# The order of the four input projections in a hybrid layer, with the state-space tables, chunk inputs and kernels moved among the products

## The chip, the cores and the metric

The kernel runs on one core of a Trainium2 chip. A core has five engines, each with its own list of instructions: TensorE (PE: matrix products and transposes, with weight loads in PEld), VectorE (DVE), ScalarE (ACT), GpSimd (POOL) and SyncE (SP, which issues the DMAs here). The metric is the device time of one execution in microseconds; of several runs the median counts.

## The reference

The program computes one layer of a streaming encoder over 1024 positions of 1024 channels in float32. What matters here is its first third:

```
h = x @ w_in                              # 1024 x 1024 @ 1024 x 2048
u, q, k, v, gate = split(h)               # 512, 256, 256, 512, 512 columns
q, k = rotary(q), rotary(k)
# state-space group: 32 groups of 16 channels, a 64-dim complex diagonal state each
bu     = einsum('blgc,gpc->blgp', u, b_bar)
states = associative_scan(a * s + bu)     # over the positions
y_s5   = rms_norm(glu(gelu(Re(C . states) + D * u)))
# retention over chunks, from q, k, v
y_ret  = group_norm(retention(q, k, v)) * silu(gate)
x = layer_norm(alpha * x + concat(y_s5, y_ret) @ w_out)
x = layer_norm(alpha * x + conv_ffn(x))
```

b_bar and the powers of the discretised state matrix are made from the parameters in the kernel. The two layer norms, the output projection and the gated MLP follow; the change does not touch them.

## The kernel before

**Products.** `w_in` is cut into four blocks of 512 columns: block 0 is u, block 1 q and k, block 2 v, block 3 the gate. Each block is one stage of `project()`. x and the weights are held as a high and a low part (an ACT cast, then a DVE subtraction that gives the rest), and each product is done three times: high by high, high by low, low by high. A stage is 8 steps over the inner dimension (k = 0 to 7, two in each of four kp), for 8 output tiles of 128 x 512 (j = 0 to 7), so 8 x 3 x 8 = 192 matmuls, one for each PSUM bank in turn. `load_w` (L168) loads a weight tile (`wraw`), casts it (L183) and splits it (L184) into one of the slots `wsp`.

**Stages in the order of before.** qk (block 1), which also loads and splits x; u (block 0), with the rotary products (L265 to L272, `rot`, `kz`) of the qk banks on DVE and their transposes (`qkt`, L276) on PE among u's products; a block of the state-space part; v (block 2); g (block 3); and then the y products (L623).

**State-space part.** DVE makes the tables: the powers of the state matrix (L331 to L409), then `W` (six instructions of 128 x 2048, L423 to L425), the end tables `ER`, `EIs` (L438 to L445). ACT and DVE copy u out of PSUM into `U` (L297), SP stores it to `uscr` and loads it back in another order as `UT`. PE transposes `W` (`bt`, L452), the copies of that are `BT` (L453), and PE multiplies `UT` by `BT` in eight groups (L461, "V groups"; L471 copies them to `V2`). A scan of seven steps over two halves follows (L501 to L514): ACT swaps the halves of the partitions (`sw`, two copies a step), DVE does four instructions. `scan_carries` (L532 to L535) is a chain of 15 steps of four small instructions, and `scan_correct` (L549 to L553) four times four instructions of 128 x 960. `short_kernel` (L478) is one small matmul for each of the 32 groups into the bank `kern`; it stands among the v products of kp 1, and `between_done` (L489) takes the bank away. As that bank is one of eight, the eighth v tile (`late`) is done afterwards for the first four k. After g, DVE makes the tables `CT` (L599 to L601), which the y products need.

**What sets the order.** The program is written as one stream; the tile framework works out the order of each engine's instructions, with the weight loads of later stages at a higher priority, and puts the semaphores between them. Each engine then runs its list as it stands. PSUM banks are taken in turn (`bank`), SBUF slots from a list of free ones (`Arena`): a tile that gets a slot waits for the last reader of the tile that had it.

Of the kernel before, what the change touches and what calls it, by code (L numbers as in the profile page):

```python
# [20 lines left out]
P = 128  # L21
# [85 lines left out]
def layer_kernel(ctx, tc, a, out):  # L107
# [40 lines left out]
    def x_parts(k):  # L148
        return [slice(0, 128), slice(128, 512), slice(512, SEQ)] if k == 0 else [slice(0, SEQ)]

# [17 lines left out]
    def load_w(blk, kp):  # L168

        n = f"wsp{blk}_{kp}"  # L170
        if blk == 1:
            load_x(kp)
        t = A.get([P, 2, 2, 512], F32R, n)
        rs = []
        for q in range(2):
            wr_n[0] += 1
            r = mp.tile([P, 512], F32, tag=f"wraw{wr_n[0] % 3}", name=f"wraw{blk}_{kp}{q}")
            SP.dma_start(r, a["w_in"][blk, :, 2 * kp + q])
            rs.append(r)
            if blk == 1:  # L180
                load_xk(2 * kp + q)
        for q, r in enumerate(rs):
            S.copy(t[:, q, 0], r)  # L183
            V.tensor_sub(t[:, q, 1], r, f32(t[:, q, 0]))  # L184
            if blk == 1:
                split_xk(2 * kp + q)
        if blk == 1:
            A.free(f"xraw{kp}")
        return t, n


    def project(blk, ops, banks, between=None, after=None, mid=None):


        ws = []
        for kp in range(4):
            with tc.high_priority(0 if blk == 1 else HP):
                w, n = load_w(blk, kp)
            late = between is not None and kp < 2
            todo = deque(between) if late and kp == 1 else ()  # L200
            ws.append(w)
            for q in range(2):
                k = 2 * kp + q
                if k < 7:
                    for (xi_, wi_) in ((0, 0), (0, 1), (1, 0)):
                        for j in range(7 if late else 8):
# [7 lines left out]
            if late:  # L214
                if kp == 0:
                    continue
                after()
                bank_n[0] -= 1
                banks[7] = bank("late")
                for k in range(4):  # L220
# [4 lines left out]
            if blk == 3:  # L225
                A.free(f"x{2 * kp}", f"x{2 * kp + 1}")
            if mid is not None and kp == 1:
                mid()

# [22 lines left out]

    banks = [bank(f"qk{b}") for b in range(8)]
    project(1, ops_b, banks)
    SP.dma_start(con, a["con"])
    SP.dma_start(ident, a["ident"])
    SP.dma_start(gains, a["gains"])
    qkT = [A.get([P, 4, 4, P], F32, f"qkT{h}") for h in range(2)]
    kz = A.get([P, 8, 256], F32, "kz")
    rot = A.get([P, 2, 2, 512], F32, "rot")  # L260
    for b in range(8):
        m1_, m2_ = rot[:, b % 2, 0], rot[:, b % 2, 1]
        cosb = con[:, C_COS + 32 * b:C_COS + 32 * b + 32].unsqueeze(1).broadcast_to([P, 16, 32])
        sinb = cust(con, C_SIN + 64 * b, [[0, 8], [32, 2], [1, 32]])
        V.tensor_mul(m1_.rearrange("p (a f) -> p a f", f=32), banks[b].rearrange("p (a f) -> p a f", f=32), cosb)  # L265
        V.tensor_mul(cust(m2_, 0, [[64, 8], [32, 2], [1, 32]]),
                     cust(banks[b], 32, [[64, 8], [-32, 2], [1, 32]]), sinb)
        V.tensor_add(m1_, m1_, m2_)
        V.tensor_mul(kz[:, b].rearrange("p (h d) -> p h d", h=4), m1_[:, 256:512].rearrange("p (h d) -> p h d", h=4),
                     con[:, C_ZETA:C_ZETA + 4].unsqueeze(2).broadcast_to([P, 4, 64]))  # L270

        V.tensor_mul(m1_[:, 0:256].rearrange("p (h d) -> p h d", h=4), m1_[:, 0:256].rearrange("p (h d) -> p h d", h=4),  # L272
                     con[:, C_XI:C_XI + 4].unsqueeze(2).broadcast_to([P, 4, 64]))
        tb = bank(f"qkt{b}")
        for e in range(4):
            T.transpose(tb[:, e * P:(e + 1) * P], m1_[:, e * P:(e + 1) * P], ident)  # L276
        S.copy(qkT[b // 4][:, b % 4], tb.rearrange("p (e k) -> p e k", e=4))  # L277
    A.free("rot")


    banks = [bank(f"u{j}") for j in range(8)]
    project(0, ops_t, banks)
    par = A.get([P, 2048], F32, "par")
    SP.dma_start(par, a["s5p"][:, 0:2048])
    pw = A.get([P, 2048], F32, "pw")
    par3 = pw[:, 1600:1696]
    SP.dma_start(par3, a["s5p"][:, 2048:S_END])

# [157 lines left out]

    BT = A.get([P, 32, P], F32, "BT")
    for q in range(8):
        b_ = bank(f"bt{q}")
        for e in range(4):  # L450
            g = 4 * q + e
            T.transpose(b_[:, e * P:(e + 1) * P], W[g // 16][:, g % 16].rearrange("p j c -> p (j c)"), ident)  # L452
        (S.copy if q % 2 else V.tensor_copy)(BT[:, 4 * q:4 * q + 4], b_.rearrange("p (g k) -> p g k", g=4))  # L453

    V2 = []
    for h in range(2):
        vb = []
        for q in range(4):
            b_ = bank(f"v{h}{q}")
            for e in range(4):  # L460
                T.matmul(b_[:, e * P:(e + 1) * P], lhsT=BT[:, 16 * h + 4 * q + e], rhs=UT[h][:, 4 * q + e],  # L461
                         start=True, stop=True)
            vb.append(b_)
        if h == 1:
            A.free("BT")
        t = A.get([P, 2, 16, P], F32, f"V2{h}")
        G.memset(t[:, 0, :, 0:1], 0.0)
        for q in range(4):
            v3 = vb[q].rearrange("p (g k) -> p g k", g=4)
            gs = slice(4 * q, 4 * q + 4)  # L470
            S.copy(t[:, 0, gs, 1:P], v3[:, :, 0:P - 1])  # L471
        V2.append(t)

    c1s = par[:, 0:512]
# [9 lines left out]
    V.tensor_mul(d3, d3, con[:, C_DM:C_DM + 16].unsqueeze(1).broadcast_to([P, NG, 16]))  # L484
    A.free("UT0", "UT1")
    tscr = dr.tile([240, 512], F32, name="tscr")
# [31 lines left out]
    def scan_carries():  # L518

        car = par[:, 0:1024].rearrange("p (z g s) -> p z g s", z=2, g=32)  # L520
        for h in range(2):
# [40 lines left out]
    vt = [A.get([P, 4, 512], F32, f"vt{h}") for h in range(2)]  # L562
    for b in range(8):
        S.copy(vt[b // 4][:, b % 4], banks[b])
    car = scan_carries()
# [38 lines left out]
    for h in range(2):  # L604
# [4 lines left out]
        TT.append(t)  # L609
    A.free("par", "pw", "scan")  # L610
    gt = [A.get([P, 4, 512], F32, f"gt{h}") for h in range(2)]
# [736 lines left out]
```

## Time and profile before

| | |
|---|---|
| runs | 1030.85, 1033.16, 1032.67 us; median 1032.67 |
| profiled execution | 1030.58 us |
| its span, first to last instruction | 1028.8 us |
| PE busy | 1003.2 us, 98% of the span |
| DVE busy | 815.4 us, 79% |
| ACT busy | 453.6 us, 44% |
| granted TensorE clock, mean | 0.996 |

The shares are means over stages with different limits. The rows below are therefore of single stretches: the part from the start to the y products is the first 214 us of the span. "x8" in a row is a count of instructions run together; a matmul whose two operands are plain fp32 stands twice in it, so the 32 matmuls of the V groups are "x64".

### The profile page before, as it was taken

How to read it: one execution, taken by the hardware profiler on the slowest of the kernel's cores; microseconds unless marked ns; L12 is line 12 of the kernel's file. 1: busy time of each engine (PE TensorE's matmuls, PEld its weight loads, DVE VectorE, ACT ScalarE, POOL GpSimd, SP SyncE). 2: the span in 40 equal slices, each digit the busy share in tenths (PEclk: the TensorE clock that was granted, in tenths of full speed). 3: DMA queues.
4: the chain of work that ended last, by engine and by line, in shares of the span. 5: the costliest groups of instructions: out<-in, count | busy, mean ns of one | idle time of the engine just before them, and what ended most of it. 6: DMA issues, size and time to landing. Idle time of an engine off the chain costs nothing.

```text
span 1028.8 us, 12777 instructions
## 1 busy us (share of the span) xinstructions
PE 1003.2 (98%) x4748; PEld 829.6 (81%) x4748; DVE 815.4 (79%) x1385; ACT 453.6 (44%) x763; POOL 50.1 (5%) x60
## 2 busy tenths in 40 slices
PE   9999899999999999999999999999999999999996
PEld 7887778887787887788888888888888888888885
DVE  5498899947775599999778778778777896759987
ACT  5121663047552147554444444444444445444800
POOL 0000000002211140000000000000000000000003
PEclk9999999999999999999999999999999999999998
DMA  8402511151212222144132232232223985643113
GB/s 285 153 1 64 193 40 54 61 206 67 98 44 102 82 103 93 52 154 144 72 128 108 74 130 103 91 114 103 106 99 143 322 323 207 233 143 123 42 41 122
DMA packets 41934, 124.05 MB, mean 121 GB/s; under 512 B 4384, under 2 KB 10912, under 8 KB 37520
## 3 DMA queue, kind: packets, MB, share of 16 engines
q1 hardware_dynamic: 41584, 122.72, 33.7%
q8 instruction: 37, 0.61, 0.2%
q10 hardware_dynamic: 288, 0.52, 0.1%
q14 instruction: 25, 0.20, 0.1%
HBM read 92.06 MB, written 31.16 MB: 120 GB/s over the span
## 4 chain that ended last, share of the span: by engine, by line
PE 82%; DVE 8%; ACT 4%; issue 2%; POOL 2%; DMA 1%; POOLq 0%; SPq 0%; DVEq 0%; ACTq 0%
PE dn L133 6%; PE dn L135 6%; PE dn L134 6%; PE u L208 4%; PE qk L208 4%; PE g L208 4%; PE v L208 1%; PE wb L133 1%; PE wb L135 1%; PE wb L134 1%; PE y L623 1%; DVE XT L1201 1%; DVE ring L976 1%; PE wo L135 1%; PE wo L133 1%
## 5 line engine op out<-in xcount | busy, mean ns | idle before, releaser
L975 ACT CAST ring<-wu 128x512 fp32r<-128x512 f32 x131 | 80.6, 620 | 145.2 <-DMA wu<-in_w_up_dram 14.5
L976 DVE TENSOR_TENSOR ring<-wu,ring 128x512 fp32r<-128x512 f32 x131 | 91.4, 702 | 21.8 <-ACT ring L975 21.8
L134 PE MATMUL dn<-ring 128*128 128x512 f32 x264 | 102.9, 390 | 0.0
L133 PE MATMUL dn<-ring 128*128 128x512 f32 x264 | 102.8, 389 | 0.0
L135 PE MATMUL dn<-ring 128*128 128x512 f32 x264 | 102.8, 389 | 0.0
L975 ACT CAST ring<-araw 128x512 fp32r<-128x512 f32 x66 | 41.1, 623 | 74.4 <-PE dn L134 61.7
L976 DVE TENSOR_TENSOR ring<-araw,ring 128x512 fp32r<-128x512 f32 x66 | 45.6, 693 | 27.6 <-ACT ring L975 27.6
L134 PEld LDWEIGHTS dn<-ring 128*128 128x128 f32 x264 | 49.6, 188 | 10.5 <-DVE ring L976 0.2
L135 PEld LDWEIGHTS dn<-ring 128*128 128x128 f32 x264 | 49.6, 188 | 10.3
L133 PEld LDWEIGHTS dn<-ring 128*128 128x128 f32 x264 | 49.6, 188 | 10.2
L976 DVE TENSOR_TENSOR ring<-wd,ring 128x512 fp32r<-128x512 f32 x66 | 45.2, 690 | 1.0 <-ACT ring L975 1.0
L975 ACT CAST ring<-wd 128x512 fp32r<-128x512 f32 x66 | 40.5, 617 | 8.2 <-DVE wd L1141 4.4
L208 PE MATMUL v<-wsp,x 128*128 128x512 f32 x147 | 42.7, 410 | 1.1 <-ACT V L471 1.1
L208 PE MATMUL qk<-wsp,x 128*128 128x512 f32 x168 | 40.8, 404 | 0.9 <-ACT x L162 0.9
L208 PE MATMUL u<-x,wsp 128*128 128x512 f32 x168 | 40.1, 394 | 0.0
L208 PEld LDWEIGHTS qk<-wsp,x 128*128 128x128 f32 x168 | 32.5, 195 | 9.1 <-ACT x L162 2.5
L208 PE MATMUL g<-wsp,x 128*128 128x512 f32 x168 | 38.2, 389 | 0.0
L208 PEld LDWEIGHTS g<-wsp,x 128*128 128x128 f32 x168 | 31.5, 188 | 6.5
L208 PEld LDWEIGHTS u<-x,wsp 128*128 128x128 f32 x168 | 30.8, 188 | 6.6 <-ACT qkT L277 0.6
L183 ACT CAST wsp<-wraw 128x512 fp32r<-128x512 f32 x32 | 19.4, 620 | 34.7 <-DMA wraw<-in_w_in_dram 23.5
L208 PEld LDWEIGHTS v<-wsp,x 128*128 128x128 f32 x147 | 27.4, 189 | 6.1 <-ACT V L471 1.9
L1068 DVE SCALAR_TENSOR_TENSOR cg<-Ab,cv,cg 128x1024 f32<-128x1024 f32 x22 | 28.3, 1285 | 4.8 <-ACT cg L1067 4.8
(1141 smaller groups left out, 2697.1 us busy)
## 6 DMA issues: line engine op xcount, KB each, us to landing
wu<-in_w_up_dram SPq DMA_DIRECT2D x22, 1024.0 KB, 4.8
araw<-hd SPq DMA_DIRECT2D x33, 512.0 KB, 3.7
wraw<-in_w_in_dram SPq DMA_DIRECT2D x32, 256.0 KB, 3.8
hd<-cg SPq DMA_DIRECT2D x22, 256.0 KB, 2.0
hd<-cg SPq DMA_DIRECT2D x11, 512.0 KB, 2.6
hd<-sS SPq DMA_DIRECT2D x11, 512.0 KB, 2.8
wd<-in_w_down_dram SPq DMA_DIRECT2D x11, 512.0 KB, 5.6
wd<-in_w_down_dram SPq DMA_DIRECT2D x22, 256.0 KB, 5.2
```

Source lines behind the costliest of these rows:

```text
L133: T.matmul(o, lhsT=lh, rhs=rh, start=first, stop=False)
L134: T.matmul(o, lhsT=lh, rhs=rl, start=False, stop=False)
L135: T.matmul(o, lhsT=ll, rhs=rh, start=False, stop=last)
L183: S.copy(t[:, q, 0], r)
L208: T.matmul(banks[j], lhsT=l, rhs=r, start=(k == 0 and xi_ == 0 and wi_ == 0), stop=False)
L623: T.matmul(o, lhsT=UT[h][:, gl], rhs=TT[h][:, :, 16 * gl:16 * gl + 16], start=True, stop=False)
L975: S.copy(t[:, 0], src)
L976: V.tensor_sub(t[:, 1], src, f32(t[:, 0]))
L1068: V.scalar_tensor_tensor(c, Ab[:, 1:1025], cv[:, f, 1:2], c, ALU.mult, ALU.add)
L1201: V.tensor_sub(lo[:, ks], src[:, ks], f32(hi[:, ks]))
```

## The change

The stages now stand in the order u, v, qk, g. x is loaded and split in the u stage, its first tile in two pieces instead of three. The constants are loaded in the middle of the u stage. The eight transposed groups of `W` and the eight V groups, which were a block of their own, now stand among the products of v, one after every fifth product: the transposes in kp 0, the V groups in kp 1. They share one PSUM bank (`small`), so v has seven banks of its own until its `late` tile; ACT alone copies them out. The kern matmuls move to kp 1 of the qk stage, and the rotary products and their transposes follow qk. `car`, the array of the carries, gets a slot of its own and no longer lies in `par`.

```diff
-        return [slice(0, 128), slice(128, 512), slice(512, SEQ)] if k == 0 else [slice(0, SEQ)]
+        return [slice(0, 512), slice(512, SEQ)] if k == 0 else [slice(0, SEQ)]
...
-    def project(blk, ops, banks, between=None, after=None, mid=None):
+    def project(blk, ops, banks, between=(), after=None, mid=None):
...
-            todo = deque(between) if late and kp == 1 else ()
+            todo = deque(between[kp]) if late and kp < 2 else deque()
...
-                after()
-                bank_n[0] -= 1
-                banks[7] = bank("late")
+                if after is not None:
+                    after()
+                banks[7] = small("late")
...
+    def small(name):
+
+        if bank_n[0] == small_n[0]:
+            bank_n[0] -= 1
+        b_ = bank(name)
+        small_n[0] = bank_n[0]
+        return b_
+
+    def spread_out(groups, n):
+
+        return [g for gr in groups for g in [gr] + [lambda: None] * (n - 1)]
...
-    banks = [bank(f"qk{b}") for b in range(8)]
-    project(1, ops_b, banks)
...
     banks = [bank(f"u{j}") for j in range(8)]
-    project(0, ops_t, banks)
...
+    project(0, ops_t, banks, mid=load_constants)
...
-    for q in range(8):
-        b_ = bank(f"bt{q}")
+    def make_BT(q):
+        b_ = small(f"bt{q}")
         for e in range(4):
...
-        (S.copy if q % 2 else V.tensor_copy)(BT[:, 4 * q:4 * q + 4], b_.rearrange("p (g k) -> p g k", g=4))
+        S.copy(BT[q // 4][:, 4 * (q % 4):4 * (q % 4) + 4], b_.rearrange("p (g k) -> p g k", g=4))
...
+    def make_V(i):
+        h, q = i // 4, i % 4
+        b_ = small(f"v{h}{q}")
+        for e in range(4):
+            T.matmul(b_[:, e * P:(e + 1) * P], lhsT=BT[h][:, 4 * q + e], rhs=UT[h][:, 4 * q + e], start=True, stop=True)
+        S.copy(V2[h][:, 0, 4 * q:4 * q + 4, 1:P], b_.rearrange("p (g k) -> p g k", g=4)[:, :, 0:P - 1])
...
+    banks = [bank(f"v_{b}") for b in range(7)] + [None]
+    project(2, ops_b, banks, [spread_out([partial(make_BT, q) for q in range(8)], 5),
+                              spread_out([partial(make_V, i) for i in range(8)], 5)])
...
-        car = par[:, 0:1024].rearrange("p (z g s) -> p z g s", z=2, g=32)
+        car = A.get([P, 1024], F32, "car").rearrange("p (z g s) -> p z g s", z=2, g=32)
...
-    banks = [bank(f"v_{b}") for b in range(7)] + [None]
-    kb = bank("kern")
-    project(2, ops_b, banks, [partial(short_kernel, g) for g in range(NG)], between_done)
...
+    banks = [bank(f"qk{b}") for b in range(7)] + [None]
+    kb = small("kern")
+    project(1, ops_b, banks, [[], [partial(short_kernel, g) for g in range(NG)]], between_done)
```

On PE, between u and v: before, the transposes (`bt`) of `W` and the V groups (`v_879` and so on, from `UT` and `BT`) stand in one block behind u's last products.

```order
L233 MATMUL u_459<-x_306,wsp_3_631 128x512 x3
L452 MATMUL bt_831<-ident,W_793 128x128 x4
L452 MATMUL bt_837<-ident,W_793 128x128 x4
L452 MATMUL bt_843<-ident,W_793 128x128 x4
L452 MATMUL bt_849<-ident,W_793 128x128 x4
L452 MATMUL bt_855<-ident,W_798 128x128 x4
```

After, on PE in the same place, each group of transposes stands between products of v (`v_505` to `v_511` are its seven banks).

```order
L208 MATMUL v_510<-wsp_0_512,x_100 128x512
L446 MATMUL bt_522<-ident,W_462 128x128 x4
L208 MATMUL v_511<-wsp_0_512,x_100 128x512
L208 MATMUL v_505<-wsp_0_512,x_100 128x512
L208 MATMUL v_506<-wsp_0_512,x_100 128x512
L208 MATMUL v_507<-wsp_0_512,x_100 128x512
L446 MATMUL bt_533<-ident,W_462 128x128 x4
```

The block is gone from PE's list; its 16 groups now have products on either side.

On ACT, at the end of the scan, before: the copies of the last scan steps (`V<-V`), then the casts of the next stage's weights (`wsp`), then the copies of v out of its banks (`vt`).

```order
L501 COPY V_925<-V_925 64x256
L502 COPY V_925<-V_925 64x256
L183 CAST wsp_0_1395<-wraw_00_1396 128x512
L183 CAST wsp_0_1395<-wraw_01_1398 128x512
L183 CAST wsp_1_1452<-wraw_10_1453 128x512
L183 CAST wsp_1_1452<-wraw_11_1455 128x512
L564 COPY vt_1297<-v_1023 128x512
```

After, on ACT at the end of the scan, where the next stage is qk and `wsp_0_947` holds its first weights.

```order
L498 COPY V_503<-V_503 64x256
L499 COPY V_503<-V_503 64x256
L470 COPY vt_837<-v_505 128x512
L470 COPY vt_837<-v_506 128x512
L470 COPY vt_837<-v_507 128x512
L470 COPY vt_837<-v_508 128x512
L470 COPY vt_838<-v_509 128x512
L470 COPY vt_838<-v_510 128x512
L470 COPY vt_838<-v_511 128x512
L183 CAST wsp_0_947<-wraw_00_948 128x512
```

The copies of v have moved ahead of the first cast for the next stage, behind the scan's last copies.

On DVE, behind the carries, before: the corrections (`scan<-par,pw`, `V<-V,scan`) follow without anything between.

```order
L535 TENSOR_TENSOR par<-par,scan 128x64
L550 TENSOR_TENSOR scan<-par,pw 128x960
L549 TENSOR_TENSOR scan<-par,pw 128x960
L551 TENSOR_TENSOR scan<-scan 128x960
L553 TENSOR_TENSOR V_899<-V_899,scan 128x8x120
L550 TENSOR_TENSOR scan<-par,pw 128x960
```

After, on DVE in the same place, where `rot` and `kz` are the rotary products from the banks `qk_939` and `qk_940`.

```order
L532 TENSOR_TENSOR car<-car,scan 128x64
L547 TENSOR_TENSOR scan<-car,pw 128x960
L546 TENSOR_TENSOR scan<-car,pw 128x960
L548 TENSOR_TENSOR scan<-scan 128x960
L566 TENSOR_TENSOR rot<-qk_939,con 128x512
L567 TENSOR_TENSOR rot<-qk_939,con 128x512
L566 TENSOR_TENSOR rot<-qk_940,con 128x512
L569 TENSOR_TENSOR rot<-rot 128x512
```

The rotary products now stand behind the carries and among the corrections.

## Rows read from the trace of the kernel before

**Rows 1.** Waits of PE: line, what it waited for, total us, times, longest

```profile
PE bt L452 <- DVE W L425: 4.7, 1, 4.7
PE late L233 <- DVE par L489: 1.9, 1, 1.9
...
PE v L208 <- ACT V L471: 1.1, 1, 1.1
```

**Rows 2.** Busy us of each engine in three stretches, with granted clock

```profile
core 0: us, PE busy (x) PEld busy (x) DVE busy (x) ACT busy (x) POOL busy (x), PEclk, DMA share, GB/s
0.00:52.00 52.00, 49.93 (x204) 39.99 (x204) 25.71 (x37) 19.53 (x27) 0.87 (x7) 1.00 0.63 217
100.00:110.00 10.00, 5.27 (x36) 5.05 (x35) 9.04 (x16) 4.46 (x8) 0.00 (x0) 0.83 0.99 332
150.00:214.00 64.00, 64.00 (x284) 52.99 (x283) 59.42 (x98) 14.53 (x25) 0.00 (x0) 1.00 0.25 87
```

**Rows 3.** PE in time order, 99 to 128: start, us, instruction, idle before

```profile
99.26 1.91 PE L452 MATMUL bt<-ident,W 128*128 128x128 f32 x16
105.90 3.27 PE L452 MATMUL bt<-ident,W 128*128 128x128 f32 x16 [4.73 <-DVE W L425]
109.01 7.31 PE L461 MATMUL v<-UT,BT 128*128 128x128 f32 x64
...
127.36 0.29 PE L478 MATMUL kern<-par,W 128*128 128x16 f32 x2
```

**Rows 4.** PE in time order, 141 to 215

```profile
141.55 3.24 PE L208 MATMUL v<-wsp,x 128*128 128x512 f32 x13
...
170.66 38.24 PE L208 MATMUL g<-wsp,x 128*128 128x512 f32 x168
...
214.18 0.38 PE L623 MATMUL y<-TT,UTb 128*128 128x128 f32 x2
```

**Rows 5.** DVE in time order, 46 to 85: rotary products, tables, W

```profile
46.89 0.69 DVE L265 TENSOR_TENSOR rot<-qk,con 128x512 f32<-128x512 f32 x1 [8.20 <-PE qk L233]
...
69.03 0.18 DVE L331 TENSOR_SCALAR scr<-pw 128x32 f32<-128x32 f32 x1 [1.30 <-PE qkt L276]
...
82.52 2.28 DVE L423 TENSOR_TENSOR W<-pw,par 128x2048 f32<-128x2048 f32 x1
```

**Rows 6.** ACT in time order, 106 to 133: casts, V copies, scan copies

```profile
106.07 0.62 ACT L183 CAST wsp<-wraw 128x512 fp32r<-128x512 f32 x1 [2.96 <-DMA uscr<-U]
...
115.34 0.66 ACT L501 COPY V<-V 64x256 f32<-64x256 f32 x1
...
118.62 2.03 ACT L471 COPY V<-v 128x508 f32<-128x508 f32 x4
...
128.81 0.68 ACT L501 COPY V<-V 64x256 f32<-64x256 f32 x1 [1.06 <-DVE V L514]
...
132.64 0.68 ACT L501 COPY V<-V 64x256 f32<-64x256 f32 x1 [1.05 <-DVE V L514]
```

**Rows 7.** DVE in time order, 145 to 212: carries, corrections, CT

```profile
145.99 0.68 DVE L489 TENSOR_TENSOR par<-par,kern 128x512 f32<-128x512 f32 x1
...
152.38 0.26 DVE L532 TENSOR_TENSOR scan<-par,pw 128x64 f32<-128x64 f32 x1
...
168.47 1.96 DVE L550 TENSOR_TENSOR scan<-par,pw 128x960 f32<-128x960 f32 x1
...
172.33 1.16 DVE L551 TENSOR_TENSOR scan<-scan 128x960 f32<-128x960 f32 x1
...
197.97 4.49 DVE L600 TENSOR_TENSOR CTt<-pw,par 128x2048 f32<-128x2048 f32 x2
...
206.78 4.49 DVE L601 TENSOR_TENSOR CT<-CT,CTt 128x2048 f32<-128x2048 f32 x2
```

**Rows 8.** PE in time order, first products and the end of qk

```profile
5.90 1.65 PE L208 MATMUL qk<-wsp,x 128*128 128x512 f32 x3 [0.53 <-ACT x L162]
7.92 1.65 PE L208 MATMUL qk<-wsp,x 128*128 128x512 f32 x3 [0.37 <-ACT x L162]
...
51.45 1.36 PE L276 MATMUL qkt<-ident,rot 128*128 128x128 f32 x8
```

More of the change, by code (lines that the diff above doesn't have):

```diff
@@ L170, in load_w @@
         n = f"wsp{blk}_{kp}"
-        if blk == 1:
+        if blk == 0:
             load_x(kp)
@@ L179, in load_w @@
             rs.append(r)
-            if blk == 1:
+            if blk == 0:
                 load_xk(2 * kp + q)
@@ L184, in load_w @@
             V.tensor_sub(t[:, q, 1], r, f32(t[:, q, 0]))
-            if blk == 1:
+            if blk == 0:
                 split_xk(2 * kp + q)
-        if blk == 1:
+        if blk == 0:
             A.free(f"xraw{kp}")
         return t, n
-    def project(blk, ops, banks, between=None, after=None, mid=None):
+    def project(blk, ops, banks, between=(), after=None, mid=None):
         ws = []
+        late = len(between) > 0
         for kp in range(4):
-            with tc.high_priority(0 if blk == 1 else HP):
+            with tc.high_priority(0 if blk == 0 else HP):
                 w, n = load_w(blk, kp)
-            late = between is not None and kp < 2
-            todo = deque(between) if late and kp == 1 else ()
+            todo = deque(between[kp]) if late and kp < 2 else deque()
             ws.append(w)
@@ L205, in project @@
                     for (xi_, wi_) in ((0, 0), (0, 1), (1, 0)):
-                        for j in range(7 if late else 8):
+                        for j in range(7 if late and kp < 2 else 8):
                             l, r = ops(w[:, q], k, j, xi_, wi_)
@@ L213, in project @@
                         proj3(banks[j], ops, w[:, q], k, j, False, True)
-            if late:
+            assert not todo
+            if mid is not None and kp == 1:
+                mid()
+            if late and kp < 2:
                 if kp == 0:
                     continue
-                after()
-                bank_n[0] -= 1
-                banks[7] = bank("late")
+                if after is not None:
+                    after()
+                banks[7] = small("late")
                 for k in range(4):
@@ L226, in project @@
                 A.free(f"x{2 * kp}", f"x{2 * kp + 1}")
-            if mid is not None and kp == 1:
-                mid()
+    small_n = [0]
+    def small(name):
[6 more added lines that the diff above has]
+        return [g for gr in groups for g in [gr] + [lambda: None] * (n - 1)]
     def proj3(o, ops, w, k, j, first, last):
@@ L250, in layer_kernel, with load_constants @@
     A.free("zero")
-    banks = [bank(f"qk{b}") for b in range(8)]
-    project(1, ops_b, banks)
[L255 to L278, printed above, removed]
     banks = [bank(f"u{j}") for j in range(8)]
-    project(0, ops_t, banks)
     par = A.get([P, 2048], F32, "par")
-    SP.dma_start(par, a["s5p"][:, 0:2048])
     pw = A.get([P, 2048], F32, "pw")
     par3 = pw[:, 1600:1696]
-    SP.dma_start(par3, a["s5p"][:, 2048:S_END])
+    def load_constants():
+        SP.dma_start(par3, a["s5p"][:, 2048:S_END])
+        SP.dma_start(con, a["con"])
+        SP.dma_start(ident, a["ident"])
+        SP.dma_start(par, a["s5p"][:, 0:2048])
+        SP.dma_start(gains, a["gains"])
+    project(0, ops_t, banks, mid=load_constants)
     uscr = dr.tile([4, P, 1024], F32, name="uscr")
@@ L445, in layer_kernel @@
     V.tensor_scalar(EIs[:, 1], EI, sgm, None, ALU.mult)
-    BT = A.get([P, 32, P], F32, "BT")
-    for q in range(8):
-        b_ = bank(f"bt{q}")
+    BT = [A.get([P, 16, P], F32, f"BT{h}") for h in range(2)]
+    def make_BT(q):
+        b_ = small(f"bt{q}")
         for e in range(4):
@@ L452, in layer_kernel @@
             T.transpose(b_[:, e * P:(e + 1) * P], W[g // 16][:, g % 16].rearrange("p j c -> p (j c)"), ident)
-        (S.copy if q % 2 else V.tensor_copy)(BT[:, 4 * q:4 * q + 4], b_.rearrange("p (g k) -> p g k", g=4))
+        S.copy(BT[q // 4][:, 4 * (q % 4):4 * (q % 4) + 4], b_.rearrange("p (g k) -> p g k", g=4))
     V2 = []
     for h in range(2):
[L457 to L465, printed above, removed]
         t = A.get([P, 2, 16, P], F32, f"V2{h}")
         G.memset(t[:, 0, :, 0:1], 0.0)
[L468 to L471, printed above, removed]
         V2.append(t)
+    def make_V(i):
[7 more added lines that the diff above has]
+                              spread_out([partial(make_V, i) for i in range(8)], 5)])
+    A.free("BT0", "BT1", "UT0", "UT1")
+    vt = [A.get([P, 4, 512], F32, f"vt{h}") for h in range(2)]
+    for b in range(8):
+        S.copy(vt[b // 4][:, b % 4], banks[b])
     c1s = par[:, 0:512]
@@ L609, in layer_kernel @@
         TT.append(t)
-    A.free("par", "pw", "scan")
+    A.free("par", "pw", "scan", "car")
     gt = [A.get([P, 4, 512], F32, f"gt{h}") for h in range(2)]
```

22 lines of the change are left out of this document (19 added, 3 removed).

## The prediction, made before the changed kernel ran

> **What bounds the kernel now.** I read the busy share first (TensorE, PE, is at work for almost the whole span), then what PE waited for, then the windows and time-ordered rows of the first 215 us. From the y products (L623) on, every engine's instructions stand in the order of before, so all that can change is when PE reaches the first of them: 214.18 [rows 4]. PE loses little ahead of it: 4.73 us before the second half of the bt transposes, 1.94 before the late products, 1.08 before a v product [rows 1, 3]. Its clock fell once: after the 4.73 us idle, 16 transposes took 3.27 us where 16 had just taken 1.91 [rows 3], and the granted clock of that window is 0.83 [rows 2], between the levels of 1.2 and 2.4 GHz. That is another 1.36; all four are 9.1 us. Behind PE stands VectorE (DVE): busy 59.42 of the 64 us from 150 to 214 [rows 2], and its last CT instruction ends at 211.27, 2.9 us before the y products [rows 7].
>
> **The prices.** The g stage's 192 products take 170.66 to 214.18, 43.5 us, 0.2267 each [rows 4]. Four transposes cost 1.91/4 = 0.48 [rows 3]. The eight V groups took 7.31, 0.91 each [rows 3]. With 32 kern matmuls among the products, 127.36 to 141.55 is 14.2 us for 31 products, so they add 7.2 [rows 3, 4]. A rope pair of banks is 20.8/4 = 5.2 us on DVE (46.89 to 67.73, where DVE's idle before 69.03 begins) [rows 5]. A pair of scan steps (both halves) is 132.64 - 128.81 = 3.83 [rows 6]; a step of one half alone is not seen before and lies between its two copies on ScalarE (ACT), 2 x 0.68, and the whole pair. I take 3.0, nearer to the pair, because its copies and its DVE instructions wait for each other in turn and only a little of the pair overlaps. Carries are 16.1 us (152.38 to 168.47); CT's six instructions are 13.3, 2.25 each (197.97 to 211.27) [rows 7].
>
> **Part 1, the start: +0.7.** The first x tile's second half came to PE at 7.92, after four products that need only the first [rows 8]. Before, the first four banks lie in that half; of u every second bank lies in the other, so one product is done, not four: 3 x 0.23. The qk stage ended at 51.45, where the qkt transposes start [rows 8]; u ends at 52.3.
>
> **Part 2, between u and v: +3.3.** The old block (bt transposes, then V groups, each waiting for a transfer) goes, and its 4.73, 1.08 and 1.36 with it. Instead the v products start behind u, with a transposed group or a V group after every fifth one. Two things can hold them. The first v weights use the slot that the last W instruction frees, and the odd copies of U on DVE stand behind all six W instructions. DVE was busy 25.71 of the first 52 us [rows 2], 5.1 of it rope; the table work of 69.03 to 82.52 and six W instructions of 2.28 add 27.2 [rows 5]. That is 47.8 of 52 us, with the constants landing only among the x loads, so I put the end of W at 51.9 and of the last U copy at 55.7: bt0 waits 2.05. Free cover gives 0 here, and a chain 5 us later gives 7. Then the casts of the second and third v weights stand on ACT behind stores of U, for which ACT waited 2.96 before [rows 6], and the BT copies behind them: 1.25 more, between 0 and 3. So the first V group comes at T0 = 52.3 + 42 x 0.2267 + 8 x 0.48 + 3.3 = 69.0.
>
> **Part 3, v: +2.0.** All groups pass through one bank and ACT alone empties it (0.51 to 0.58 a copy, the four in 2.03 [rows 6]); five products, 1.14 us, cover that. What is left is the fixed order among scan copies: I charge 0.4, 0.95, and 0.7 before late (ends 0 and 4). From T0: 150 products, 34.0, eight groups, 7.3, and 2.05: v ends at T0 + 43.4 = 112.4. The 1.94 of late <- par goes, since late no longer takes the kern bank.
>
> **Part 4, the scan is behind: +8.6 and 1.4.** The scan started at 115.34 [rows 6], and all of the v products behind it were its cover. Now its first half cannot start before the fourth V group and the other before the eighth. Order: T0 + 17.5 for the eighth copy, 2.7 for two pairs of sw copies, 3 x 3.83, then 4 x 3.0 for the second half alone, and about 3.8 for four casts and four splits that stand in between: T0 + 47.6. Next on ACT come seven vt copies and only then the cast of the first qk weights, which PE needs: 7 x 0.52 (four V copies took 2.03 [rows 6]) and 0.62. So qk starts at S = T0 + 52.0 = 121.0, 8.6 us after v ended. Before, the casts of the next stage stood ahead of the vt copies. At 1.9 for a single step the wait is 4; at 3.83, 12.
>
> On rows alone ACT and DVE run in the order of the program: kern was ready at 141.55, yet L489, behind the scan's steps on DVE, ran at 145.99 [rows 4, 7]. The Trainium skill, "TensorE: Matmul & The Clock Gate", section "Architectural detail: the array is 16× 32×32, not 1× 128×128", says that ScalarE and VectorE are strictly first-in first-out while TensorE can pull weight loads ahead; that rule speaks against this change, the trace agrees, and without it the cast would pass the scan and this term would be nil.
>
> An idle stretch of 8.6 us is longer than the 4.73 after which the clock was seen at its lower level, so I charge the same 1.4 once. The Trainium skill, on that page in the section "What's actually happening", has the clock as one of two states set by how busy TensorE has lately been; by it the price is per fall, by a price in proportion to idle time it would be 1.4 x 8.6/4.7 = 2.6, and the trace has one fall only, so cannot tell.
>
> **Part 5, rope and DVE's backlog: +9.9.** qk takes 43.5 + 7.2 + 1.4 from S, and 0.2 for its first product: it ends at Q = S + 52.3 = 173.3. Before, rope started 4.6 us before qk's end (46.89 against 51.45) and DVE had nothing else. Now car has a slot of its own, the one that qk's late products give up, so the carries start at S + 30.5; 16.1 of carries, 1.3 of copies into car, 0.6 of one more split and three instructions of the corrections (5.1: two of 1.96 and one of 1.16 [rows 7]) precede rope: it starts at S + 53.6, Q + 1.3. Corrections and splits for 7.5 us stand between its pairs: it ends 28.3 later, S + 81.9. PE's order holds 116 of g's 192 products behind the last qkt, 26.4 us: y starts not before S + 108.8. Counted by DVE: from the carries to CTt's end 47.8 before, 20.8 of rope and 1.2 of splits beside them put the split of g's last weights at S + 100.3, and 40 products need it: S + 109.4. Without these waits y would be at Q + 43.5 + 8 x 0.46 = S + 99.5 (the eight qkt groups stand in this stretch too, and 0.46 takes them a little under the bt transposes' 0.48); the difference is 9.9. The backlog on DVE was hidden before because rope was done at 67.7; the cover is gone when it shares 60 us with the corrections. If rope goes first, this is 0 to 5; if g's weights are late too, 13.
>
> **The sum.** -9.1 + 0.7 + 3.3 + 2.0 + 8.6 + 1.4 + 9.9 = +16.8; place by place, y at 121.0 + 109.4 = 230.4, +16.2. I take the second. The profiled execution took 1030.58, its span 1028.8 and 1.8 around it; 1046.8 there. The median of the runs, 1032.67, is 2.1 above that execution: 1048.9.
>
> **Rivals.** A, faster: the waits of before go with the lost clock and no new one bites: 16.2 - 8.6 - 1.4 - 9.9 - 3.3 = -7.0, 1025.7. For it: the removed waits are real, and PE's own work hardly changes. It holds if the scan ends by T0 + 39, rope starts 4 us before Q and W ends before u; against it stand ACT's order and 59.42 of 64 busy on DVE. 0.08. B, only one of the two new waits: the scan's (with DVE's backlog hidden) or the backlog (with the cast in time): 16.2 - 10 in either case, +6.2, 1039. For it: the step of one scan half alone is an estimate. Against it: the two rest on different engines, and each has its own order. 0.21. C, no change: neither in full, half of the backlog left: 16.2 - 10 - 5 = +1.2, 1034. 0.06. D, more: W ends 3 us later and the clock falls a second time before g (by the above PE waits some 5 us for qkt0): 16.2 + 3 + 1.4 = 20.6, 1053.3. For it: W's end is an estimate with 47.8 of 52 us full. 0.1.
>
> **Chances and range.** The forecast, 1045 to 1052 by itself, has 0.55. A difference under 0.2%, 2 us, cannot be told from none. Faster is A, 0.08; same is C, 0.06; slower is the forecast, B and D, 0.86. The range, 1036 to 1054, leaves out A, C and a bit of B and D.
>
> **What would show it.** In the profile after: PE idle of some 8 us between the last v product and the first qk product, released by ACT's cast of qk weights; a granted clock below 1 just after it; rope's first instruction on DVE after qk's end, with gaps in g released by rope or a split; no wait of bt for W over 3 us; y's first product near 230. Wrong it is if the scan's last copies come before v's last product, or if y starts before 222.

## The result and the profile after

The changed kernel takes 1049.09 us, median of four runs (1048.63 to 1050.08); the kernel before, timed beside it, 1031.76 (1029.92 to 1033.16). The ratio is 1.0168, interval 1.0153 to 1.0183: slower by 17.3 us. The forecast was 1048.9 and slower. The profiled execution took 1050.08 with a span of 1048.3, against 1030.58 and 1028.8. Its y products start at 233.12, those of before at 214.18 [rows 4]: 18.9 of the 19.5 us by which the span grew lie ahead of them, as the prediction had it.

What PE waited for in the kernel after (what waited, what it waited for: us in total, times, longest):

```profile
PE qk L208 <- ACT wsp L183: 7.7, 1, 7.7
PE qkt L577 <- DVE rot L573: 4.9, 1, 4.9
PE v L208 <- ACT wsp L183: 2.6, 1, 2.6
...
PE v L460 <- ACT V L461: 1.1, 2, 0.7
PE g L208 <- ACT qkT L578: 1.1, 2, 0.7
PE v L208 <- DVE U L290: 0.8, 1, 0.8
```

The three waits of [rows 1] are gone, and each of the three new ones at the top stands at a stage's border: v's first weights, qk's first weights, the first rotary transpose. PE in order of time (start, duration, instruction, idle before it):

```profile
5.13 4.25 PE L208 MATMUL u<-x,wsp 128*128 128x512 f32 x16 [0.18 <-ACT x L162]
...
51.90 1.51 PE L208 MATMUL v<-wsp,x 128*128 128x512 f32 x5 [2.62 <-ACT wsp L183]
...
69.55 1.05 PE L460 MATMUL v<-UT,BT 128*128 128x128 f32 x8
...
112.42 0.84 PE L248 MATMUL late<-wsp,x 128*128 128x512 f32 x3
120.98 12.07 PE L208 MATMUL qk<-wsp,x 128*128 128x512 f32 x43 [7.72 <-ACT wsp L183]
...
173.28 0.84 PE L248 MATMUL late<-wsp,x 128*128 128x512 f32 x3
179.03 1.09 PE L577 MATMUL qkt<-ident,rot 128*128 128x128 f32 x4 [4.91 <-DVE rot L573]
180.79 3.78 PE L208 MATMUL g<-wsp,x 128*128 128x512 f32 x8 [0.68 <-ACT qkT L578]
...
223.90 3.94 PE L208 MATMUL g<-wsp,x 128*128 128x512 f32 x16 [0.31 <-DVE wsp L184]
...
233.12 0.44 PE L639 MATMUL y<-TT,UTb 128*128 128x128 f32 x2
```

The first rows answer to [rows 8], where PE waited a second time at 7.92; here sixteen products run through (each row counts what ran together without a listed wait). ACT at the end of the scan:

```profile
115.58 0.64 ACT L498 COPY V<-V 64x256 f32<-64x256 f32 x1 [1.60 <-DVE V L511]
116.23 0.64 ACT L499 COPY V<-V 64x256 f32<-64x256 f32 x1
116.90 3.52 ACT L470 COPY vt<-v 128x512 f32<-128x512 f32 x7
120.25 1.20 ACT L183 CAST wsp<-wraw 128x512 fp32r<-128x512 f32 x2
```

This is the chain of Part 4: the last scan copy, seven copies of v, and only then the cast that PE waits for, although the last three v products end at 113.26 (112.42 + 0.84). DVE behind the carries:

```profile
152.40 0.41 DVE L519 COPY car<-V 128x256 f32<-128x256 f32 x1 [4.44 <-PE late L248]
...
170.25 1.94 DVE L547 TENSOR_TENSOR scan<-car,pw 128x960 f32<-128x960 f32 x1
...
175.14 0.68 DVE L566 TENSOR_TENSOR rot<-qk,con 128x512 f32<-128x512 f32 x1
...
185.46 0.69 DVE L566 TENSOR_TENSOR rot<-qk,con 128x512 f32<-128x512 f32 x1 [1.83 <-PE qkt L577]
...
223.17 1.28 DVE L184 TENSOR_TENSOR wsp<-wraw,wsp 128x512 fp32r<-128x512 f32 x2
```

The carries wait for the slot that qk's late products free (152.40), so rope starts 1.0 after qk's end (174.12) instead of 4.6 before it, and the last g weights are split at 223.17, forty products before y. Windows of the kernel after, with columns as in [rows 2]; the granted clock is the number behind POOL:

```profile
51.00:62.00 11.00, 9.30 (x32) 7.14 (x33) 9.85 (x31) 5.01 (x9) 0.00 (x0) 0.69 0.84 240
113.00:133.00 20.00, 12.28 (x47) 9.77 (x45) 5.69 (x10) 9.77 (x18) 0.00 (x0) 0.83 0.21 68
173.00:193.00 20.00, 13.97 (x53) 10.69 (x53) 17.90 (x29) 3.36 (x6) 0.00 (x0) 0.74 0.08 26
```

PE's clock was between 1.2 and 2.4 GHz on the mean in three stretches, one behind each of the three waits; before, in one [rows 2].

### The profile page after: what moved, and what is told of

Read it like the earlier page. It is cut to its first block, busy times and chain, and to the rows that moved or that the text cites. A ratio compares the mean times of both kernels' runs of the same rounds, so it can differ in the third digit from the quotient of the medians.

```text
span 1048.3 us, 12762 instructions
## 1 busy us (share of the span) xinstructions
PE 1011.4 (96%) x4748; PEld 832.1 (79%) x4748; DVE 812.2 (77%) x1380; ACT 454.0 (43%) x766; POOL 50.4 (5%) x60
## 4 chain that ended last, share of the span: by engine, by line
PE 54%; DVE 5%; issue 2%; POOL 1%; ACT 1%; POOLq 0%; DVEq 0%
PE dn L135 6%; PE dn L134 6%; PE dn L133 6%; DVE ring L992 1%; DVE XT L1217 1%; POOL zw L852 1%; DVE lbsf L862 0%; POOL lrsa L845 0%; DVE zw L1282 0%; POOL lrsb L845 0%; DVE zw L1289 0%; DVE xt L917 0%; ACT zw L851 0%; ACT z L851 0%; DVE XB L1217 0%
## 5 line engine op out<-in xcount | busy, mean ns | idle before, releaser
L208 PE MATMUL qk<-wsp,x 128*128 128x512 f32 x147 | 44.4, 425 | 7.7 <-ACT wsp L183 7.7
L208 PE MATMUL g<-wsp,x 128*128 128x512 f32 x168 | 44.1, 415 | 2.0 <-ACT qkT L578 1.1
L208 PEld LDWEIGHTS qk<-wsp,x 128*128 128x128 f32 x147 | 29.1, 199 | 13.1 <-ACT wsp L183 8.1
L184 DVE TENSOR_TENSOR wsp<-wraw,wsp 128x512 fp32r<-128x512 f32 x32 | 21.2, 687 | 19.9 <-ACT wsp L183 19.9
```

## The experiments

The theory of the forecast is two waits on separate engines, the scan on ACT (Part 4) and DVE's backlog (Part 5), each worth about 10 us. Rivals: one of the two hides the other, so that taking away either gives nothing or everything; or the time lies in something else, such as the clock or the start. Each ratio is to the kernel before, run on the same chip; differences in microseconds are of medians where nothing else is said, and medians of before differ by a microsecond or so between chips. By the ratios the differences are up to 1.3 us larger or smaller.

**e1: the carries' slot.** The tile `car` is asked for before the qk banks, so it gets a slot that is free; the slots of what is asked for behind it move too.

```
+    car_t = A.get([P, 1024], F32, "car")
     banks = [bank(f"qk{b}") for b in range(7)] + [None]
-        car = A.get([P, 1024], F32, "car").rearrange(...)
+        car = car_t.rearrange(...)
```

> The changed kernel, with the array of the carries in a slot that is free before qk's weights are loaded, so that carries and corrections can run during the qk products. Theory (VectorE's backlog behind a late car holds rope, and rope holds g): the carries start right after the scan, rope starts before the end of qk, the wait of qkt for rot (4.9 us), the small waits in g (2.0) and the half-clock stretch behind them (some 3) go. The slots move too: the cast of the first qk weights no longer waits for v's last slot, and only the copies of v stand behind the scan's last steps, so the 7.7 us wait should shrink to about 4. Together -10 and -3.5: 1035 to 1037. Rival (g is held by its own late weights or by the clock, not by rope): only the 3.5 goes, 1045.

Measured: 1039.31, ratio 1.0061 (1.0041 to 1.0081). First PE, then DVE, of e1:

```profile
121.05 12.42 PE L208 MATMUL qk<-wsp,x 128*128 128x512 f32 x41 [0.49 <-ACT vt L470]
...
174.38 1.36 PE L578 MATMUL qkt<-ident,rot 128*128 128x128 f32 x8
```
```profile
169.81 0.69 DVE L567 TENSOR_TENSOR rot<-qk,con 128x512 f32<-128x512 f32 x1 [3.60 <-PE qk L248]
```

The casts of qk's weights now run ahead of the vt copies, but the scan still holds the banks: PE waits for three vt copies (5.4 in all), and the rest of qk starts at 121.05, as late as before the edit. Rope starts ahead of qk's end, and the 4.9 of qkt is gone. So nearly all of the 9.8 us it gives (11.0 by the ratios) is Part 5's: from qk's end to y it takes 10.7 less in the profiles. It came out 2.3 us above the range expected.

**e2: a short scan.** Steps 4 to 7 are left out.

```
-        for j in range(1, 8):
+        for j in range(1, 4):
```

> The changed kernel with three scan steps of each half left out of six... that is, steps 1 to 3 run and steps 4 to 7 do not (the result is not the scan's). Nothing else moves. Theory (the first qk cast stands behind the scan on ScalarE): the scan ends before v's last product, the wait of 7.7 us before qk falls to about 1 (the cast behind v's last slot, 0.6, and hand-overs) and the clock does not fall there, 2.3: 1049 - 9 = 1040. The waits in g stay as they are (4.9 for rot). Rival (the wait belongs to the slot and the copies of v, whatever the scan does): the wait stays over 5 us, 1047 or more.

Measured: 1040.4, ratio 1.0073 (1.0057 to 1.0088). PE of e2 at the qk stage's start:

```profile
113.83 10.04 PE L208 MATMUL qk<-wsp,x 128*128 128x512 f32 x43 [0.75 <-ACT wsp L183]
```

The wait of 7.72 is 0.75, and the same 43 products take 10.04 instead of 12.07. The wait of 4.9 for rope stays. So 8.7 us (9.8 by the ratios) belong to the scan, 9.8 to the backlog, and neither hides the other: 18.5 together, against the 17.3 by which the change is slower. As this kernel also leaves out work of DVE, e5 has to show that the wait goes with the whole scan done.

**e3: the start alone, in the kernel before.**

```
-        return [slice(0, 128), slice(128, 512), slice(512, SEQ)] if k == 0 else [slice(0, SEQ)]
+        return [slice(0, 512), slice(512, SEQ)] if k == 0 else [slice(0, SEQ)]
```

> The kernel before, with the first x tile in two pieces of 512 columns instead of three; nothing else. In the changed kernel the first stage ran without waits from 5.13 us and ended 2.2 us earlier than qk did before, where I had forecast 0.7 later. Theory: one DMA issue less (0.43 us on SyncE) and larger pieces bring the second half 2.5 us earlier, and the whole program moves up by 2.0 to 2.8: 1029. Rival (u's products, not the loads, made the start faster; or the gain is lost at the next wait for a load): 1031 to 1032.

Measured: 1030.21, ratio 0.9976 (0.9966 to 0.9987): faster by 1.8 by the medians, 2.5 by the ratio. ACT in e3, then in the kernel before:

```profile
4.59 0.62 ACT L162 CAST x<-xraw 128x512 fp32r<-128x512 f32 x1
6.25 0.62 ACT L162 CAST x<-xraw 128x512 fp32r<-128x512 f32 x1 [1.03 <-DMA xraw<-in_xT_dram]
```
```profile
5.34 0.51 ACT L162 CAST x<-xraw 128x384 fp32r<-128x384 f32 x1 [0.92 <-DMA xraw<-in_xT_dram]
7.25 0.62 ACT L162 CAST x<-xraw 128x512 fp32r<-128x512 f32 x1 [1.40 <-DMA xraw<-in_xT_dram]
```

With two pieces the second half is cast at 6.25, with three at 7.25: the number of pieces decides when the half that Part 1 waits for lands. By the medians the gain is a little less than the 2.0 to 2.8 expected. In the profiled execution qk ends 1.8 earlier (49.65), but y starts at 214.31, against 214.18 before, since the clock was low for longer behind later waits (12 late products took 4.39, before 3.02); so the gain is shown by the runs' times alone.

**e4: the scan's swap copies on GpSimd.**

```
-        S.copy(sw[0:64], cur[64:128])
-        S.copy(sw[64:128], cur[0:64])
+        G.tensor_copy(sw[0:64], cur[64:128])
+        G.tensor_copy(sw[64:128], cur[0:64])
```

> The changed kernel with the two half-swapping copies of every scan step on GpSimd instead of ScalarE; the results are the same. Theory (ScalarE's order is what holds qk): ScalarE has only the copies of v ahead of the first qk cast, so the first qk product waits about 1 us instead of 7.7. But the split of those weights on VectorE still stands behind the scan, and the eighth qk product needs it: if a GpSimd copy takes no longer than ScalarE's 0.68, 1040; at 1.4 each the scan ends some 10 us later than now and PE waits at the eighth product instead of the first, 1049 to 1053. Rival (the scan's length on VectorE and not ScalarE's order is the bound): the wait moves to the split even at equal copies, 1046 or more.

Measured: 1051.63, ratio 1.0176 (1.0158 to 1.0195). POOL, then PE, of e4:

```profile
92.54 0.92 POOL L498 COPY V<-V 64x256 f32<-64x256 f32 x1
...
108.23 0.96 POOL L498 COPY V<-V 64x256 f32<-64x256 f32 x1 [2.37 <-DVE V L511]
```
```profile
115.02 3.21 PE L208 MATMUL qk<-wsp,x 128*128 128x512 f32 x7 [4.95 <-ACT wsp L183]
123.48 10.98 PE L208 MATMUL qk<-wsp,x 128*128 128x512 f32 x36 [5.25 <-DVE wsp L184]
```

A copy takes 0.63 to 1.12 on POOL, 0.64 to 0.70 on ACT; a step of one half alone takes 3.3 instead of 3.0, and the scan ends at 124.98 instead of 116.87. The cast is earlier (114.29), but the split of its weights stands on DVE behind the slower scan: the wait of 7.72 has become 4.95 and 5.25. An engine that is free doesn't help a chain of dependent steps if each step is longer there.

**e5: the last swaps of the second half on DVE**, where each takes 0.38 to 0.41.

```
+        eng = V.tensor_copy if h == 1 and j >= 4 else S.copy
+        eng(sw[0:64], cur[64:128])
+        eng(sw[64:128], cur[0:64])
```

> The changed kernel with the half-swapping copies of the second half's steps 4 to 7 on VectorE instead of ScalarE (same results; car still late). Theory (ScalarE's order is what holds qk, not the scan's own length): the copies of v and the first qk cast no longer stand behind the scan's last steps, though the whole scan is still done; the wait before qk falls from 7.7 us to 1 or 2, its half-clock stretch (2.3) goes, the waits in g stay: 1039 to 1041. Rival (what is gained by leaving steps out, 8.7 us, came from less work on VectorE): the time stays above 1045.

Measured: 1042.29, ratio 1.0107 (1.0089 to 1.0125). PE, then DVE, of e5:

```profile
114.21 1.89 PE L208 MATMUL qk<-wsp,x 128*128 128x512 f32 x7 [0.75 <-ACT wsp L183]
117.73 8.48 PE L208 MATMUL qk<-wsp,x 128*128 128x512 f32 x36 [1.62 <-DVE wsp L184]
```
```profile
116.57 0.38 DVE L500 COPY V<-V 64x256 f32<-64x256 f32 x1
```

The whole scan is done, and it is no shorter: its last copy ends at 116.95, after the change at 116.87. Yet the wait is 2.4 in two pieces. So what held qk was not the scan's length by itself but ACT's order, in which the copies of v and the cast stand behind the scan's last copies; e2 took the wait away by ending those sooner. The 1.62 that is left is the split on DVE, which still stands behind the scan. It came out 1.3 above the range; the v stage's first wait was 3.6 here.

**e6: e1 and e5 together.**

> The changed kernel with both edits: car in a slot free early, and the second half's last four swaps on VectorE. Theory (two separate causes that add): from the 1039.3 of car alone the 5.4 us of waits for the copies of v and some 2.5 of half clock behind them go, 1031 to 1032, that is the time of the kernel before, while this kernel still has the small waits between u and v (2.7) and among the V groups (2.4). Rival (the causes share the time, so that the second edit finds little): 1036 or more.

Measured: 1037.19, ratio 1.0059 (1.0041 to 1.0078): 5 us above what the sum gives. PE of e6:

```profile
146.46 5.49 PE L248 MATMUL late<-wsp,x 128*128 128x512 f32 x12 [4.57 <-DVE par L486]
```

A new wait: the kern bank's sum (L486) on DVE now stands behind corrections that run early, and the late products need that bank; their 12 take 5.49 where 2.88 is seen without a wait (e8). That is the wait of before [rows 1], longer.

**e7: e6, U copied by ACT alone, BT in another slot.**

```
-                (S.copy if e == 0 else V.tensor_copy)(t[:, c, :, e * 64:(e + 1) * 64], src)
+                S.copy(t[:, c, :, e * 64:(e + 1) * 64], src)
...
+    A.free_n[0], A.free_n[2] = A.free_n[2], A.free_n[0]
     BT = [A.get([P, 16, P], F32, f"BT{h}") for h in range(2)]
```

> The last kernel, and all eight copies of U on ScalarE instead of four behind the six W instructions on VectorE, with the first v weights in the slot that the table's scratch gives up instead of W's temporary. Theory (between u and v PE waits for W's end by way of U's copies and of the weight slot): 0.8 to 3.4 us of waits at the first v products go, and with them a half-clock stretch where there is one: 1028 to 1030. Rival (those waits are set by when W itself is done, so bt waits instead; or the stores of U are later and the second weights wait): within 1 us of the last kernel.

Measured: 1035.1, ratio 1.0044 (1.0032 to 1.0057), 5 above the range. v's first products no longer wait (which of the two edits did it, no run tells), but the waits of e7 are now these:

```profile
PE late L248 <- DVE par L487: 4.4, 1, 4.4
PE bt L447 <- ACT BT L448: 3.6, 3, 1.4
```

The first is e6's, untouched. The second is Part 2's other wait: two casts of v's weights wait 1.36 and 1.71 on ACT for stores of U, and BT copies stand behind each.

**e8: e7, and ACT empties the kern bank** into free columns of `car`, before DVE adds it.

```
-        V.tensor_add(drep, drep, kb)
+        S.copy(car_t[:, 1024:1536], kb)
+        V.tensor_add(drep, drep, car_t[:, 1024:1536])
```

> The last kernel, with the kern bank copied out by ScalarE (into the free half of car's slot) instead of read by VectorE behind the carries and corrections. Theory (what the early car gained came back as a wait of qk's late products for the kern bank, 4.4 us, and a clock fall behind it, some 3): both go, 1035.1 - 7 = 1028. Rival (the next stage is held by VectorE anyway, so that the time comes back as a wait for rope): 1033 or more.

Measured: 1031.80, ratio 0.9998 (0.9989 to 1.0008), 3.8 above what was expected. The wait of `late` is gone and with it 4.7 us by the ratios (1.0044 to 0.9998); the bt waits stay, and one for rope of 2.6, in two pieces, comes in behind.

**e9: e8, and the first half's early swaps on DVE too.**

```
-        eng = V.tensor_copy if h == 1 and j >= 4 else S.copy
+        eng = V.tensor_copy if (h == 1 and j >= 4) or (h == 0 and j < 4) else S.copy
```

> The kernel of the run before it, and the swaps of the first half's steps 0 to 3 on VectorE too, so that ScalarE has nothing between the copies of the V groups. Theory (the one rotating bank makes PE wait for ScalarE's copies when scan copies stand between): the waits among the V groups and before v's late products, 2.5 us, go: 2 to 2.5 below the run before. Rival (VectorE's longer list ends the scan later and something behind it waits): within 1 of it, or above.

Measured: 1031.84, ratio 0.9999 (0.9990 to 1.0008): nothing. The V groups' waits go, but rope's wait grows from 2.6 to 3.4 (the second figure of a row is the number of waits, the third the longest):

```profile
PE bt L447 <- ACT BT L448: 3.5, 4, 1.5
PE qkt L581 <- DVE rot L577: 3.4, 2, 2.6
```

By these rows DVE is the bound from the scan to rope, so work brought to it is paid there.

**e10: e9, and the splits of qk's weights from kp 1 on and of g's first on GpSimd; e11: `kz` as well.** They ask whether POOL can relieve DVE. The diff of e10 (in e11 `V.tensor_mul(kz...` is `G.tensor_mul` too):

```
-            V.tensor_sub(t[:, q, 1], r, f32(t[:, q, 0]))
+            (G if (blk == 1 and kp > 0) or (blk == 3 and kp == 0) else V).tensor_sub(t[:, q, 1], r, f32(t[:, q, 0]))
```

> The kernel of the early swaps, with the splits of qk's weights for kp 1 to 3 and of g's first weights (eight instructions of 0.69 us) on GpSimd instead of VectorE. Theory (what still holds the changed order is VectorE's list ahead of rope: PE waits 3.4 us for rot): 5.5 us less ahead of rope takes that wait and the clock fall behind it away, 1031.8 - 4 = 1028. Rival (GpSimd is slow enough, at 1.07 us for a swap copy, that the low parts of the weights come late): waits of qk products for them, 1032 or more.

> The run before it, and kz (eight instructions of 0.42 us among rope's) on GpSimd too. Theory: rope's pairs fall from 5.2 to 4.4 us on VectorE; if qkt no longer waits for rot this gives nothing (within 1 us of the run before), if it still waits, up to 0.8. Rival (rope's two buffers are freed only when GpSimd has read them): a wait of rope for kz, 1 to 3 us more.

Measured: e10 1033.24, ratio 1.0019 (1.0010 to 1.0027); e11 1032.88, 1.0011 (1.0002 to 1.0021): e10 is slower than e9, and e11 not faster. POOL and DVE of e10, then DVE of e9:

```profile
110.60 1.28 POOL L184 TENSOR_TENSOR wsp<-wraw,wsp 128x512 fp32r<-128x512 f32 x1 [1.99 <-ACT wsp L183]
...
110.75 1.62 DVE L514 TENSOR_TENSOR V<-V,scan 128x256 f32<-128x256 f32 x1
```
```profile
110.80 0.64 DVE L514 TENSOR_TENSOR V<-V,scan 128x256 f32<-128x256 f32 x1
```

The same DVE instruction takes 1.62 beside POOL's split and 0.64 without; it ends (112.37) half a microsecond behind the split (111.88). The 1.0 lost is more than the 0.6 to 0.7 that the split costs on DVE. PE's wait for rope fell only from 3.4 to 2.9, and the one for the copies of v ahead of qk rose from 0.5 to 1.6; no qk product waited for a split on POOL, which was the rival's mechanism. The Trainium skill, "SBUF — State Buffer", section "Who interferes with whom", says that a VectorE instruction with two SBUF inputs contends with a GpSimd one that reads SBUF; the trace agrees.

**e12: e9, the casts of v's second and third weights on DVE, and the UT loads ahead of weight loads on SP.** This takes the casts from in front of the BT copies.

```
-            S.copy(t[:, q, 0], r)
+            (V.tensor_copy if blk == 2 and kp in (1, 2) else S.copy)(t[:, q, 0], r)
...
+        with tc.high_priority(2 * HP):
+            UT.append(load_UT(h, f"UT{h}"))
```

> The kernel of the early swaps (splits back on VectorE), with the casts of v's second and third pair of weights (kp 1 and 2, four instructions) on VectorE instead of ScalarE, and UT's two loads ahead of the weight loads behind them on SyncE. Theory (between u and v, ScalarE's copies of BT stand behind casts that wait for the stores of U, and PE waits 3.5 us for those copies): the first V group comes at 64 to 65 us instead of 68, all of it reaches the y products, 1031.8 - 3 = 1028 to 1029. Rival (UT's load or the stores are what the first V group waits for, or the time comes back as a longer wait for rope): within 1 us of 1031.8.

Measured: 1028.52, ten runs, ratio 0.9968 (0.9957 to 0.9979). The bt waits are 1.0 and the first V group runs at 64.98, against 69.55 after. It beats both kernels, by 3 us the one before. What it still pays is rope, with the clock low behind that wait:

```profile
64.98 1.05 PE L462 MATMUL v<-UT,BT 128*128 128x128 f32 x8
...
162.20 1.08 PE L582 MATMUL qkt<-ident,rot 128*128 128x128 f32 x4 [2.66 <-DVE rot L578]
```
```profile
160.00:166.00 6.00, 3.49 (x12) 2.84 (x13) 5.96 (x13) 1.98 (x4) 0.00 (x0) 0.66 0.14 46
```

It also pays some 1.6 us that no list of waits shows: the first qk products come one by one behind the copies that empty v's banks, so the 43 up to the first kern matmul take 11.5 at a granted clock of 1.00, in e2 9.9.

If the shorter start is worth here what it is in e3, it makes up 1.8 of the 3.0 us (2.5 of 3.3 by the ratios). The new order by itself, with these waits treated, is then worth about 1 us, which can't be told from nothing. That is a difference of two runs: no kernel has the new order with the old start.

## Why the prediction was right

The two big terms were right in kind, place and size. Part 1 was wrong by 3 us, and the next stretch took that up again, for a reason that Part 2 holds. Place by place, stretch by stretch:

| stretch | predicted | measured | off |
|---|---|---|---|
| start to u's end | 52.3 | 49.28 (51.90 - 2.62) | -3.0 |
| u's end to the first V group | 16.7 | 20.27 | +3.6 |
| to v's end (113.26) | 43.4 | 43.71 | +0.3 |
| to qk's start | 8.6 | 7.72 | -0.9 |
| qk's start to its end (174.12) | 52.3 | 53.14 | +0.8 |
| qk's end to y | 57.1 | 59.00 | +1.9 |

*Part 1 failed: +0.7 forecast, -2.2 measured.* (Its sum for u's end is also off by a little: 51.45 and 0.69 make 52.1, not 52.3.) The working took the arrival of x's second half from before, 7.92 [rows 8], as given, and only asked which products need it. The diff shows three pieces becoming two; the arrival moved with them (e3). The size is that of one execution: e1, e2, e4 and e5 run the same instructions in the same order up to 69 us, and there u ended between 49.33 and 51.89.

*Part 2 came out in time (69.55, 69.0 forecast), though not by its sum.* W ended at 51.15 (51.9 forecast) and the last copy of U at 54.75 (55.7). PE's waits, 2.62 and 0.80 against 3.3, all stood at the first v products and none at the BT copies. Behind them the clock fell, to a mean of 0.69 from 51 to 62, and no term priced that: the same work takes 16.85 here (17.65 from 51.90 to 69.55, less 0.80) and 13.69 in e12 at full clock (50.26 to 64.98, less a wait of 1.03), 3.2 us more. But neither this nor the earlier u decided when the first V group came. PE of e1:

```profile
46.29 5.60 PE L248 MATMUL u<-x,wsp 128*128 128x512 f32 x24
...
60.83 0.66 PE L446 MATMUL bt<-ident,W 128*128 128x128 f32 x4 [0.98 <-ACT BT L447]
...
69.29 1.05 PE L460 MATMUL v<-UT,BT 128*128 128x128 f32 x8
```

The window from 52 to 70, first of the kernel after, then of e1:

```profile
52.00:70.00 18.00, 17.20 (x80) 13.58 (x81) 10.26 (x31) 8.21 (x15) 0.00 (x0) 0.81 0.93 298
52.00:70.00 18.00, 15.22 (x82) 11.49 (x83) 10.28 (x31) 8.12 (x15) 0.00 (x0) 1.00 0.94 295
```

In e1 u ended 2.6 later (51.89) and the clock stayed full, yet the V group came at 69.29: PE waited for BT instead, 0.98 and 0.89. In e4 the two are 51.15 and 68.86. So the chain of W, U, casts and BT copies on DVE and ACT set the time, as Part 2 had it, and what u gained was waited away; e12, which takes the casts out of that chain, has the V group at 64.98. The table's first two errors are therefore one error and its echo, not two that cancelled by chance.

*Part 3 held:* 1.66 in three waits (0.46, 0.69, 0.51), 2.0 forecast.

*Part 4 held: 8.6 and 1.4 forecast, 7.7 and 2.0 measured* (43 products from 120.98 to the first kern matmul at 132.90, against 113.83 to 123.71 in e2). The step that decided it, 3.0 for a scan step of one half alone, is 2.9 in the trace (L498 at 112.64 and 115.58). The scan ended at 116.87, and T0 + 47.6 is 117.15. e2 takes the term away and gives 8.7 with 0.75 of wait left.

*Part 5 held: 9.9 forecast, 9.8 given back by e1 (11.0 by the ratios).* The bound is DVE, as the prediction counted it: last split at S + 102.2 (S + 100.3 forecast), then forty products, 9.95 to y. PE's listed waits in that stretch are 4.91, 0.68, 0.45, 0.56 and 0.31, or 6.9. The third low clock costs PE 3.7: 13.23 us from 179.03 to 192.26 for 29 products (6.6), four groups (1.8) and 1.1 of waits. Part of that reached y by way of DVE, which waits 1.83 and 0.23 for qkt in this stretch, since rot's two buffers come free only when PE has transposed them; that is about the 1.9 by which the last split missed its forecast. e2 bears it out: behind the same wait of 4.9 the same products take 12.18, 1.05 less, DVE waits 1.41, and from the first qkt to y it takes 53.25 instead of 54.09.

*The rivals.* B was wrong of this change, which paid both waits, but its price was right for a kernel with one of them: e1 and e2 measured 1039.3 and 1040.4, B said 1039. A failed on ACT's order, as argued against it: the cast did not pass the vt copies. D's second fall of the clock came, and a third, but W was not late. That the median was met to 0.2 us is luck: y came 2.7 later than forecast (233.12 against 230.4), and the profiled execution, 3.3 above the forecast's 1046.8, was the slowest of its four, while the 2.1 added for the median came from a profiled execution of before that was faster than all three runs.

*The clock's price.* The prediction took one price per fall, 1.4 [rows 3]. The runs show that PE lost 3.2 behind idle stretches of 2.62 and 0.80, 2.1 behind 2.75 in the same place in e2, 2.0 behind 7.72, and 3.0 behind 4.57 (e6: 12 products in 5.49 against 2.88 in e8, and the next seven in 2.09 against 1.75). So the price doesn't grow with the idle time, and one figure for each fall isn't it either. Nor is PE's loss always the kernel's, as Parts 2 and 5 show. The Trainium skill, "TensorE: Matmul & The Clock Gate", section "What's actually happening", has two states of the clock; the trace agrees, with a granted clock of 0.50 from 179 to 186, behind the wait for rope, and 1.00 from 193 to 213, but no fixed price follows from that.

## What to carry to other kernels

When a stage moves, ask for each engine's chain what it was hidden behind and what now stands at the border of the stage; two chains on different engines then have separate prices, and taking away one shows the other's in full. A stage that is done earlier gains nothing where the next one hangs on another engine's chain: u ended 2.6 us apart in two runs, and the first V group came within 0.3. Behind each wait that is removed, look for the next in the same list: here most repairs uncovered one (kern bank, BT copies, rope), and it took six kernels from e1 on to get from +17 to -3 us. Price a low clock behind every new wait of some microseconds, ask whether PE is what the stretch hangs on, and don't take the arrival of a load from before when the diff changes how it is cut.

## What the runs showed of the hardware that was not expected

- A tensor-tensor instruction on GpSimd lengthens VectorE's beside it: L514 1.62 against 0.64 (e10 and e9); the correction L550 took 3.06 in e11 beside two splits on POOL, against 1.96 in e9. A swap copy with one input (L501) took 1.23 beside a split in e10, against 0.41 in e9.
- The swap copy of 64 x 256 between partition halves takes 0.38 to 0.43 on VectorE (e5, e9), 0.64 to 0.70 on ScalarE (the kernel after), 0.63 to 1.12 on GpSimd (e4).
- A wait of 2.62 us, with another of 0.80 close behind it, was followed by a lower clock that cost PE more (3.2) than the one behind 7.72 (2.0). In e1 the same place had waits of 0.80, 0.98 and 0.89, and the granted clock stayed at 1.00.
